# An encoder block on one core: transposed input, a late token factor for the first projections, and convolution weights split by adding transfers

## The chip, the cores and the metric

The kernel runs on one core of one Trainium2 chip, as one program. Its time is the device time of that core in microseconds (us). Three runs of the kernel before gave 2022.7, 2023.65 and 2024.65, so the median is 2023.65 us.

In the profile PE is TensorE's matmuls and PEld its weight loads, DVE is VectorE, ACT ScalarE, POOL GpSimd, SP SyncE. `L94` is line 94 of the kernel.

## What is computed

One layer on x of 512 tokens by 1024 channels, all in float32:

```
h   = x + Mixer(RMSNorm(x))
h   = h + PEER(RMSNorm(h))
out = RMSNorm_final(h)
```

The mixer multiplies the normalised x with one wide matrix `w_in` of 10,240 columns. Its columns go to a gated recurrence (HGRN2, 5 x 1024 columns), to a long convolution (Hyena: x0, x1 and v, 3 x 1024) and to two branch gates (2 x 1024). What this change touches is the norm, the convolution and one block of the second gate:

```python
def rmsnorm(x, g):
    y = xf * lax.rsqrt(jnp.mean(xf * xf, axis=-1, keepdims=True) + RMS_EPS)
    return y * g

proj = jnp.einsum('bld,dc->blc', xn, w_in)
q, zf_fwd, zf_bwd, inp, og, hy, gates = jnp.split(proj, IN_SPLITS, axis=-1)
hy = centred_short_conv(hy, conv_w, conv_b)
x0, x1, v = jnp.split(hy, 3, axis=-1)
y_b = x0 * bidirectional_fftconv(v * x1, h_f, h_b, hyena_bias)
```

The filters h_f and h_b come from a small network of sines. PEER is a product-key retrieval over 16,384 experts and takes the second half of the time; the change leaves its code alone.

## The kernel before

Numbers are held as a sum of two short ones: a high part that TensorE multiplies in one pass (dtype fp32r) and a low part, the residual. `split` (L91) makes them: ScalarE casts the high part, VectorE subtracts. `mm3` (L97) then multiplies high by high, low by high and high by low. A projection (`proj`, L144) computes 128 columns of `w_in` for all 512 tokens: `load_w` (L133) fetches a 512 KB weight block over SyncE's queue, splits it, and `product` (L149) runs 24 matmuls of 128x512 into one of three PSUM banks, named `ps_mm`.

**The start** (`mixer`, L217). x comes in four tiles of 128 tokens. For each, ScalarE squares it with a sum per token (`token_rstd`, L941), VectorE multiplies the tile with the token's factor and with the norm's gain, which TensorE had spread over the partitions (L243), and `turn` (L198) transposes it on TensorE, eight transposes per tile, and splits the result into `xh` and `xl`, the normalised input with channels on the partitions. The first two projections (`proj_halves`, L157) run on halves of the tokens between the transposes, 256 columns per matmul.

**The convolution** (`hyena`, L348). The 1024 channels go through in four rounds of 256, called `half` in the code. A round makes three projections for each of its two blocks of 128 channels: x1 (block 8 on), v (16 on) and x0 (0 on). `conv` (L374) is the centred short convolution on the projection's result: one ScalarE and two VectorE operations (L377 to L379), which also set the PSUM bank free. x1 times v is folded into `sd` (L539 to L543) and transposed on TensorE (L546, L558). `filtered` (L462) makes the round's filter, folds it (L493 to L509) and returns it; `parted` (L512) splits it into f0 and f1. `spectrum` (L574) multiplies with tables (`tco`, `tso`, ...), which come as transfers on GpSimd's queue that cast to fp32r (L398), each behind a copy of one column on ScalarE (L397), by which the moment of the transfer is set. Then come the products of the spectra, the way back and the multiplication with x0 (L648). Projections of the second gate fill in: `gates_b` (L261) yields one at a time.

**What sets the order.** The code is written stage by stage, and a scheduler puts the instructions of each engine into one row, in which they wait for each other's results. An engine takes its row strictly in that order; a transfer stands in the row of the engine that issues it. A tile of a pool can be filled again only when everything that used it is done. The weights had three raw tiles and two each for the high and the low part.

The lines that the prediction speaks of: L94 (the residual), L102 to L105 (`mm3`), L243, L250, L379, L398, L505 to L509, L546.

Of the kernel before, what the change touches and what calls it, by code (L numbers as in the profile page):

```python
# [9 lines left out]
F32 = mybir.dt.float32  # L10
# [31 lines left out]
for _n, _w in (("lb0", 8), ("lb1", 8), ("hg", 1), ("cw0", 24), ("cw1", 24), ("cw2", 24),  # L42
               ("cb", 24), ("f_b1", 1), ("f_q1", 1), ("f_b2", 1), ("f_q2", 1), ("negt", 4)):
    VEC[_n] = (_o, _w)
    _o += _w
# [80 lines left out]

def fetch_w(C, src):
    raw = C.wraw.tile([P, KB, P], F32, name="wraw")
    C.nc.sync.dma_start(raw, src)
    return raw  # L130


def load_w(C, src, raw=None, eng=None):  # L133
# [10 lines left out]
def proj(C, src, xh, xl, eng=None):  # L144

    return product(C, load_w(C, src, eng=eng), xh, xl)


def product(C, w, xh, xl):  # L149

    hi, lo = w
    ps = C.ps_mm.tile([P, L], F32, name="ps_mm")
    mm3(C.nc, ps, [((hi[:, k], lo[:, k]), (xh[:, k], xl[:, k])) for k in range(KB)])
    return ps

# [16 lines left out]
def block_kernel(tc, a):  # L172

    nc = tc.nc
    with ExitStack() as ctx:
# [5 lines left out]
        nc.scalar.dma_start(ident, a["ident"])  # L181
        epsc = const.tile([P, 1], F32, name="epsc")
        nc.vector.memset(epsc, EPS)
        C = Ctx()
        C.fetch_vec = lambda: nc.scalar.dma_start(vec, a["vec"])
# [27 lines left out]
FIRST_CONV = (8, 16)  # L213
# [3 lines left out]
def mixer(C):  # L217
# [3 lines left out]
    C.wraw = wctx.enter_context(tc.tile_pool(name="wraw", bufs=3))  # L221
    C.whi = wctx.enter_context(tc.tile_pool(name="whi", bufs=2))
# [7 lines left out]
    with tc.tile_pool(name="norm", bufs=1) as n1, tc.tile_pool(name="norm2", bufs=TB) as n2:  # L230
        log_table(C)
        C.fetch_vec()
        gm = n1.tile([1, D], F32, name="gm")
        gps = [C.ps_x.tile([P, 512], F32, name="ps_x") for _ in range(2)]
        xns, raws = [], []
        for tb in range(TB):
            xn = n2.tile([P, D], F32, name="xn")
            nc.sync.dma_start(xn, a["x"][tb * P : tb * P + P])
            xns.append(xn)
            if tb == 0:  # L240
                nc.scalar.dma_start(gm, a["g_mix"])
                for c, pg in enumerate(gps):
                    nc.tensor.matmul(pg, C.ones[0:1], gm[:, c * 512 : c * 512 + 512], start=True, stop=True)  # L243
            elif tb < 3:
                raws.append(fetch_w(C, a["w_in"][40 + FIRST_CONV[tb - 1]]))
        for tb, xn in enumerate(xns):
            rs = token_rstd(C, n2, xn, "nrs")
            for c, pg in enumerate(gps):
                xc = xn[:, c * 512 : c * 512 + 512]
                nc.vector.scalar_tensor_tensor(xc, xc, rs, pg, op0=ALU.mult, op1=ALU.mult)  # L250
            turn(C, xn, xh, xl, tb)
    rctx = ExitStack()
    branch = rctx.enter_context(tc.tile_pool(name="branch", bufs=1, side="right"))
    C.yb = mg = branch.tile([P, KB, L], F32, name="yb")
    gctx = ExitStack()
# [5 lines left out]
    def gates_b():  # L261
        w = None
        for db in range(KB):
# [11 lines left out]
    fill = gates_b()  # L275
    with ExitStack() as c2:
        hyena(C, c2, xh, xl, raws, fill)
# [51 lines left out]
def load_wo(C, pool, c):  # L329
# [7 lines left out]
    raw = C.wraw.tile([P, KB, P], F32, name="wraw")  # L337
    nc.sync.dma_start(raw, C.a["w_o"][c])
# [9 lines left out]
def hyena(C, ctx, xh, xl, raws, fill):  # L348
# [7 lines left out]
    w2 = ctx.enter_context(tc.tile_pool(name="hyw", bufs=2))  # L356
    HC = 256
# [13 lines left out]

    first = dict(zip(FIRST_CONV, proj_halves(C, (None, None), xh, xl, raws=raws)))

    def conv(dst, blk):  # L374

        ps = first.pop(blk, None) or proj(C, a["w_in"][40 + blk], xh, xl)
# [6 lines left out]
    alt = cp.tile([P, H + 2], F32R, name="alt")  # L383
    altc = cp.tile([P, 1], F32R, name="altc")

    def setup(steps):
# [7 lines left out]
        nc.sync.dma_start(fw2, a["f_w2"])  # L394
        for (name, w), step in zip(TABLES, steps):
# [66 lines left out]
    def filtered(half):  # L462

        hb = w2.tile([1, HC], F32, name="hb", bufs=1)
        nc.sync.dma_start(hb, a["hb"][:, half * HC : half * HC + HC])
        fw3 = w2.tile([2 * FH, 2, HC], F32, name="fw3", bufs=1)
# [3 lines left out]
        fw3h = w2.tile([2 * FH, 2, HC], F32R, name="fw3h", bufs=1)  # L470
        fw3l = w2.tile([2 * FH, 2, HC], F32R, name="fw3l", bufs=1)
# [3 lines left out]
        decb = w2.tile([P, 2, HC], F32, name="decb", bufs=1)  # L475
# [5 lines left out]
        pm_ = w2.tile([P, 2, 4, HC], F32, name="pm", bufs=1)  # L481
        for t in range(TB):
            win = w2.tile([P, 2, HC], F32, name="win")
# [8 lines left out]
            nc.vector.tensor_sub(pm_[:, 1, t], win[:, t // 2], win[:, 1 - t // 2])  # L492
        near, apart = pm_[0:1, 0], pm_[0:1, 1]  # L493
# [1134 lines left out]
```

## Time and profile before

The profiled execution took 2022.85 us, 0.8 less than the median of the runs. Its span, from the first to the last instruction, is 2021.1 us; 1.75 us lie around it.

| | us |
|---|---|
| median of 3 runs | 2023.65 |
| profiled execution | 2022.85 |
| its span | 2021.1 |
| mean granted TensorE clock | 0.995 |
| TensorE waiting for VectorE at L379, once | 7.1 |
| TensorE waiting before its first instruction | 6.1 |
| wlo, the weights' residuals on VectorE (112 in all) | 136.4 |

How to read it: a row of the waits names the engine and line that waited and what it waited for, with the total, the number of times and the longest. A table of stretches gives the busy time of each engine in each, with the number of instructions, then the clock that TensorE was granted (1.00 is full speed), the share of the transfer engines that was busy and what they moved. A row of the timeline has the start, the duration, the engine and line, what is written from what, and in brackets the idle time before it with what ended it. Matmuls overlap, so that 24 of 0.39 us follow each other at 0.227.

### The profile page before, as it was taken

What the parts mean: (1) busy time and instruction counts of PE and PEld (TensorE: products, weight loads), DVE (VectorE), ACT (ScalarE), POOL (GpSimd) and SP (SyncE); (2) the same over time, 40 slices, a digit from 0 to 9 for tenths busy, and PEclk for the clock granted to TensorE, in tenths of its full rate; (3) what the DMA queues carried; (4) which work ended last, traced back from release to release, by engine and by line L of the source; (5) the groups of instructions that cost most, each with busy time, mean ns of one, the idle gap of its engine ahead of it and who ended that gap; (6) DMA issues with size and microseconds to landing.
All of it is one profiled execution on the core that took longest, in us unless ns stands there. A gap on an engine that the chain in (4) does not pass through costs nothing.

```text
span 2021.1 us, 32312 instructions
## 1 busy us (share of the span) xinstructions
PE 1992.0 (99%) x12417; PEld 1760.2 (87%) x12417; DVE 1659.1 (82%) x2971; ACT 989.3 (49%) x1466; POOL 564.6 (28%) x338
## 2 busy tenths in 40 slices
PE   7989999999999999999999999999999999999998
PEld 6878888888888898889999998888888888888887
DVE  5799863889987737979999968877888889888995
ACT  5645453777775624436767643333333333333333
POOL 0000000000000000000000037777767767676760
PEclk9989999999999999999999999999999999999999
DMA  6412123222222434224767998889989899899984
GB/s 192 133 62 84 69 100 103 85 74 75 74 74 75 146 127 155 90 79 165 227 200 233 282 339 331 326 330 326 352 320 336 333 354 342 334 335 332 336 305 152
DMA packets 161683, 423.60 MB, mean 210 GB/s; under 512 B 12917, under 2 KB 64889, under 8 KB 161402
## 3 DMA queue, kind: packets, MB, share of 16 engines
q1 hardware_dynamic: 117176, 267.03, 37.9%
q0 software_dynamic: 37872, 137.91, 18.8%
q10 hardware_dynamic: 6482, 16.61, 2.4%
q8 instruction: 97, 1.59, 0.3%
q14 instruction: 56, 0.46, 0.1%
HBM read 381.92 MB, written 39.58 MB: 209 GB/s over the span
## 4 chain that ended last, share of the span: by engine, by line
PE 94%; DVE 4%; ACT 1%; DMA 1%; issue 1%; SPq 0%; DVEq 0%; ACTq 0%
PE ps_mm L105 10%; PE ps_mm L102 10%; PE ps_mm L103 10%; PE acc L1192 9%; PE acc L1191 9%; PE acc L1190 9%; PE ps_a L102 9%; PE ps_a L103 9%; PE ps_a L105 8%; PE ps_g L1477 4%; PE ps_x L748 1%; PE ps_x L102 1%; PE ps_x L105 1%; PE ps_x L103 1%; PE ps_s L1322 1%
## 5 line engine op out<-in xcount | busy, mean ns | idle before, releaser
L94 POOL TENSOR_TENSOR ul<-uraw,uh 128x1024 fp32r<-128x1024 f32 x70 | 186.7, 2667 | 576.1 <-PE ps_a L105 436.3
L102 PE MATMUL ps_a<-pxh,uh 128*128 128x384 f32 x1024 | 345.8, 338 | 0.3 <-ACT gact L1042 0.3
L103 PE MATMUL ps_a<-pxl,uh 128*128 128x384 f32 x1024 | 342.3, 334 | 0.0
L1192 PE MATMUL acc<-vh,gl 128*128 128x512 f32 x768 | 300.7, 392 | 0.0
L1191 PE MATMUL acc<-vl,gh 128*128 128x512 f32 x768 | 300.0, 391 | 0.0
L1190 PE MATMUL acc<-vh,gh 128*128 128x512 f32 x768 | 299.2, 390 | 0.0
L102 PE MATMUL ps_mm<-xh,whi 128*128 128x512 f32 (+1 forms) x656 | 257.8, 395 | 7.1 <-DVE x L379 7.1
L93 ACT CAST vh<-vraw 128x1024 fp32r<-128x1024 f32 x128 | 134.6, 1052 | 256.5 <-PE acc L1192 137.2
L103 PE MATMUL ps_mm<-xl,whi 128*128 128x512 f32 (+1 forms) x656 | 255.4, 391 | 0.0
L1145 DVE SCALAR_TENSOR_TENSOR xg<-grow,gw,xg 128x1024 f32<-128x1024 f32 x127 | 201.8, 1589 | 27.4 <-DMA grow<-in_v,gidx 25.8
L1133 DVE SCALAR_TENSOR_TENSOR grow<-grow,xg 128x1024 f32<-128x1024 f32 x128 | 187.0, 1480 | 44.9 <-DMA grow<-in_u,gidx 44.6
L1104 POOL DMA_INDIRECT grow<-in_u,gidx x128 | 198.5, 1551 | 36.4 <-issue 22.9
L105 PE MATMUL ps_a<-pxh,ul 128*128 128x384 f32 x1024 | 198.4, 334 | 0.0
L102 PEld LDWEIGHTS ps_a<-pxh,uh 128*128 128x128 f32 x1024 | 192.4, 188 | 3.7 <-ACT gact L1042 0.6
L103 PEld LDWEIGHTS ps_a<-pxl,uh 128*128 128x128 f32 x1024 | 192.4, 188 | 3.7
L1013 POOL IOTA iota<- 128x512 bf16 x1 | 1.2, 1190 | 691.4 <-PE ps_mm L105 691.4
L93 ACT CAST uh<-uraw 128x1024 fp32r<-128x1024 f32 x128 | 134.7, 1052 | 119.7 <-PE ps_a L103 83.2
L94 DVE TENSOR_TENSOR wlo<-wraw,whi 128x1024 fp32r<-128x1024 f32 x112 | 136.4, 1219 | 68.8 <-ACT whi L93 39.4
L94 DVE TENSOR_TENSOR vl<-vraw,vh 128x1024 fp32r<-128x1024 f32 x128 | 186.8, 1460 | 6.2 <-ACT vh L93 6.2
L1104 POOL DMA_INDIRECT grow<-in_v,gidx x128 | 174.2, 1361 | 36.7 <-issue 20.9
L105 PEld LDWEIGHTS ps_a<-pxh,ul 128*128 128x128 f32 x1024 | 179.3, 188 | 0.0
L93 ACT CAST whi<-wraw 128x1024 fp32r<-128x1024 f32 x112 | 117.3, 1048 | 120.6 <-PE ps_mm L103 108.1
(427 smaller groups left out, 3952.3 us busy)
## 6 DMA issues: line engine op xcount, KB each, us to landing
uraw<-in_uT SPq DMA_DIRECT2D x128, 512.0 KB, 5.7
vraw<-in_v SPq DMA_DIRECT2D x128, 512.0 KB, 6.0
wraw<-in_w_in SPq DMA_DIRECT2D x80, 512.0 KB, 3.3
Gd<-Gs SPq DMA_DIRECT2D x12, 2048.0 KB, 10.1
gt<-Gd SPq DMA_DIRECT2D x32, 768.0 KB, 7.8
kept<-gact ACTq DMA_DIRECT2D x22, 384.0 KB, 2.9
gkept<-kept SPq DMA_DIRECT2D x22, 384.0 KB, 5.6
wraw<-in_w_q SPq DMA_DIRECT2D x16, 512.0 KB, 4.2
```

Source lines behind the costliest of these rows:

```text
L93: nc.scalar.copy(hi, src)
L94: return (eng or nc.vector).tensor_sub(lo, src, hi).ins
L102: nc.tensor.matmul(out, ah, bh, start=(i == 0), stop=False)
L103: nc.tensor.matmul(out, *((al, bh) if late else (ah, bl)), start=False, stop=False)
L105: nc.tensor.matmul(out, *((ah, bl) if late else (al, bh)), start=False, stop=(stop and i == n - 1))
L1104: nc.gpsimd.indirect_dma_start(out=t, out_offset=None, in_=tab, in_offset=bass.IndirectOffsetOnAxis(ap=gidx[:, j : j + 1], axis=0))
L1133: nc.vector.scalar_tensor_tensor(t, t, 1.0, xg, op0=ALU.mult, op1=ALU.mult, accum_out=gdot[h][:, i : i + 1])
L1145: nc.vector.scalar_tensor_tensor(gacc, t, gw[h][:, i : i + 1], gacc, op0=ALU.mult, op1=ALU.add)
L1190: nc.tensor.matmul(acc[k][c], gh[:, ts_], vh[:, ds_], start=(r == 0), stop=False)
L1191: nc.tensor.matmul(acc[k][c], gh[:, ts_], vl[:, ds_], start=False, stop=False)
L1192: nc.tensor.matmul(acc[k][c], gl[:, ts_], vh[:, ds_], start=False, stop=(r == NK - 1))
L1477: nc.tensor.matmul(pg[:, q * P : q * P + P], own[:, q], rows[:, q], start=True, stop=True)
```

## The change

Eight things change, three of them large.

1. **The input comes transposed as well** (`xT`, laid out on the host), in eight slices of 128 channels by 512 tokens. There are no transposes in the mixer any more. The new function `begun` scales each slice with the norm's gain alone (`gm`, one number per channel) and splits it into `uh` and `ul`.
2. **The first five projections multiply `uh` and `ul`** and get the token's factor `rs` afterwards, by one multiplication of the result. They are the first block of the second gate, which stood in the first round, and the four convolution blocks of the list `FIRST_CONV`: 8, 16, 0 and 9. The factor comes from the sum of the squares of the slices, made by ScalarE and VectorE and summed over the partitions by one fp32 matmul with ones (L259). Meanwhile VectorE and ScalarE make `xh` and `xl` from the slices for all later projections. The results lie in `yb`, which the convolution fills only later: the gate's is stored from there, and `conv` reads the other four.
3. **The convolution's weights are split by transfers.** While `C.cast` is set, a transfer on GpSimd's queue casts the weight into the high part (L145), ScalarE writes its negative into the low part (L146), and a second transfer of the same 512 KB adds the weight to it (L147). VectorE has no part in it. After the convolution weights are split as before.
4. The pools of raw, high and low tiles become one ring of seven tiles of the same size. A raw tile takes the place of a low part of three weights before.
5. The folding of the filter (`folded_filter`) is cut from `filtered` and done where its result is split, so in the next round behind the convolutions.
6. The alternating signs come cast on GpSimd's queue too, and the tables' marker copies read other tiles.
7. `ident` is fetched later, some tiles of `hyena` lie in a pool of their own.
8. The halves of the first two projections are gone: all matmuls of a projection have 512 columns.

The core of the difference:

```diff
 def load_w(C, src, raw=None, behind=None):
     nc = C.nc
+    if raw is None and C.cast:
+        hi, lo = w_tile(C, "whi"), w_tile(C, "wlo")
+        if behind is not None:
+            nc.scalar.copy(hi[:, 0, 0:1], behind)
+        nc.gpsimd.dma_start(hi, src)
+        nc.scalar.mul(lo, hi, -1.0)
+        nc.gpsimd.dma_start(lo, src, accum_op=ALU.add)
+        return hi, lo
     if raw is None:
         raw = fetch_w(C, src)
-    hi = C.whi.tile([P, KB, P], F32R, name="whi")
-    lo = C.whi.tile([P, KB, P], F32R, name="wlo")
-    split(nc, hi, lo, raw, eng)
+    hi, lo = w_tile(C, "whi"), w_tile(C, "wlo")
+    split(nc, hi, lo, raw)
     return hi, lo
...
+def begun(C, xh, xl):
...
+        raw, w = w_tile(C, "wraw", F32), (w_tile(C, "whi"), w_tile(C, "wlo"))
+        for k in range(KB):
+            if k in (0, KB // 2):
+                ks = slice(k, k + KB // 2)
+                nc.sync.dma_start(raw[:, ks], a["w_in"][72][:, ks])
+                split(nc, w[0][:, ks], w[1][:, ks], raw[:, ks])
+            nc.sync.dma_start(xT[:, k], a["xT"][:, k])
+        later = fetch_w(C, a["w_in"][40 + FIRST_CONV[0]])
+        C.fetch_ident()
+        for k in range(KB):
+            g = vcol(C, "gm", k)
+            nc.scalar.activation(uh[:, k], xT[:, k], AF.Identity, scale=g)
+            nc.vector.scalar_tensor_tensor(ul[:, k], xT[:, k], g, uh[:, k], op0=ALU.mult, op1=ALU.subtract)
+        gate0 = product(C, w, uh, ul, C.ps_x, "ps_x")
+        made = {}
+        w = load_w(C, None, later)
+        total = sp.tile([P, L], F32, name="total", bufs=1)
+        nc.scalar.activation(total, xT[:, 0], AF.Square)
+        for k in range(1, KB):
+            sq = sp.tile([P, L], F32, name="sq")
+            nc.scalar.activation(sq, xT[:, k], AF.Square)
+            nc.vector.tensor_add(total, total, sq)
+        ms = C.ps_x.tile([P, L], F32, name="ps_x")
+        nc.tensor.matmul(ms, C.ones, total, start=True, stop=True)
+        rstd_from(C, rs, ms, 1.0 / D)
+        for i, blk in enumerate(FIRST_CONV):
+            if i:
+                w = load_w(C, a["w_in"][40 + blk], behind=xT[:, KB - 1, 0:1])
+            made[blk] = product(C, w, uh, ul)
...
+                nc.vector.tensor_mul(yb[:, 3 + i], made[blk], rs)
...
+        evict(0)
+        for k in range(KB):
+            nc.vector.scalar_tensor_tensor(xT[:, k], xT[:, k], vcol(C, "gm", k), rs, op0=ALU.mult, op1=ALU.mult)
+            C.turned = nc.scalar.copy(xh[:, k], xT[:, k]).ins
+            nc.vector.tensor_sub(xl[:, k], xT[:, k], xh[:, k])
+        evict(1)
+    return evict, gate0
-FIRST_CONV = (8, 16)
+FIRST_CONV = (8, 16, 0, 9)
...
-    C.wraw = wctx.enter_context(tc.tile_pool(name="wraw", bufs=3))
-    C.whi = wctx.enter_context(tc.tile_pool(name="whi", bufs=2))
+    C.ring = wctx.enter_context(tc.tile_pool(name="weights", bufs=7))
+    C.cast = True
...
+        return lambda: folded_filter(pm_, hb)
...
         if half == 1:
-            fe, fo = parted(*folded)
+            fe, fo = parted(*rest())
...
-        if half < 2:
+        if half == 1:
             next(fill)
```

The rows of three engines show what the scheduler made of it. First ScalarE at the start. Before, casts of the transposed input (`xh`) stand between the squares of the tiles (`junk`):

```order
L124 ACTIVATE nrs<-nrs 128x1
L93 CAST whi<-wraw 128x1024
L209 CAST xh<-ps_x 128x4x128
L945 ACTIVATE junk,nrs<-xn 128x1024
L209 CAST xh<-ps_x 128x4x128 x3
L123 ACTIVATE nrs<-nrs,epsc 128x1
```

Now, behind the last scaled slice (`sq` is a slice's square, `whi<-xT` the marker of a cast transfer, `wlo<-whi` the negative, `yb` the token factor's logarithm, L123, and exponential, L124):

```order
L247 ACTIVATE uh<-xT,vec 128x512 x3
L256 ACTIVATE sq<-xT 128x512 x2
L93 CAST whi<-wraw 128x1024
L256 ACTIVATE sq<-xT 128x512
L144 CAST whi<-xT 128x1
L256 ACTIVATE sq<-xT 128x512 x2
L146 ACTIVATE wlo<-whi 128x1024
L123 ACTIVATE yb<-ps_x,epsc 128x512
L144 CAST whi<-xT 128x1
L124 ACTIVATE yb<-yb 128x512
L276 CAST xh<-xT 128x512
L448 COPY signs<-xh 128x1
```

The negative of the first cast weight, which needs that weight's transfer, stands ahead of the token factor and of the next weight's marker. Second, GpSimd, whose row in the convolution held the seven tables:

```order
L398 DMA tco<-in_tco 128x1024
L398 DMA tso<-in_tso 128x1024
L398 DMA tee<-in_tee 128x1024
L398 DMA tceT<-in_tceT 128x1032
L398 DMA tsoT<-in_tsoT 128x1032
```

Now the cast (L145) and adding (L147) transfers stand between them, with numbers to tell the weights apart:

```order
L145 DMA whi_216<-in_w_in 128x1024
L147 DMA wlo_217<-in_w_in 128x1024
L145 DMA whi_247<-in_w_in 128x1024
L449 DMA signs_352<-in_alt 128x259
L453 DMA tco_512<-in_tco 128x1024
L147 DMA wlo_248<-in_w_in 128x1024
L145 DMA whi_278<-in_w_in 128x1024
L453 DMA tso_515<-in_tso 128x1024
L145 DMA whi_410<-in_w_in 128x1024
L147 DMA wlo_279<-in_w_in 128x1024
```

The high part of a later weight stands ahead of the low part of an earlier one: 410 ahead of 279. Third, VectorE at the end of the first round and in the second. Before, the folding of the next filter (`pm_875`, `once_919`) stands ahead of the convolutions of the second block (`x1_1129`, `vv_1131`, out of the PSUM banks 1138 and 1172):

```order
L505 TENSOR_TENSOR once_919<-pm_875 128x1024
L554 TENSOR_TENSOR tw_1084<-ps_x_1075,far_1082 128x2x128
L506 TENSOR_TENSOR pm_875<-pm_875 128x2x512
L94 TENSOR_TENSOR uel_996<-tw_1084,ueh_995 128x4x128
L508 TENSOR_TENSOR pm_875<-once_919 128x2x256
L509 TENSOR_TENSOR pm_875<-once_919 128x2x256
L370 TENSOR_TENSOR um_322<-ps_x_1090,um_322 1x128
L378 SCALAR_TENSOR_TENSOR x1_1129<-ps_mm_1138,vec_61,x1_1129 128x511
L378 SCALAR_TENSOR_TENSOR vv_1131<-ps_mm_1172,vec_61,vv_1131 128x511
L379 SCALAR_TENSOR_TENSOR x1_1129<-ps_mm_1138,vec_61,x1_1129 128x511
L379 SCALAR_TENSOR_TENSOR vv_1131<-ps_mm_1172,vec_61,vv_1131 128x511
L94 TENSOR_TENSOR wlo_1230<-wraw_1227,whi_1229 128x1024
```

Now the same block's convolution (`vv_1045`, out of bank 1084) comes first:

```order
L609 TENSOR_TENSOR tw_999<-ps_x_990,far_997 128x2x128
L432 SCALAR_TENSOR_TENSOR vv_1045<-ps_mm_1084,vec_61,vv_1045 128x511
L703 TENSOR_TENSOR yb_87<-yconv_903,x0_469 128x512
L94 TENSOR_TENSOR uel_913<-tw_999,ueh_912 128x4x128
L590 TENSOR_TENSOR x1_1043<-vv_1045,x1_1043 128x512
L431 SCALAR_TENSOR_TENSOR x0_1138<-ps_mm_1144,vec_61,x0_1138 128x511
```

and the folding (`pm_808`, `once_1182`) follows 20 rows further on, right ahead of the split of the filter (`f1l`, `f0l`) for the next spectrum:

```order
L560 TENSOR_TENSOR once_1182<-pm_808 128x1024
L561 TENSOR_TENSOR pm_808<-pm_808 128x2x512
L563 TENSOR_TENSOR pm_808<-once_1182 128x2x256
L564 TENSOR_TENSOR pm_808<-once_1182 128x2x256
L94 TENSOR_TENSOR f1l_1191<-pm_808,f1h_1190 128x1024
L94 TENSOR_TENSOR f0l_1189<-pm_808,f0h_1188 128x1024
```

The folding has moved behind the convolutions, and no residual of a weight (`wlo`) is left in this part of VectorE's row.

More of the change, by code (lines that the diff above doesn't have):

```diff
@@ L184, in block_kernel @@
         C = Ctx()
+        C.fetch_ident = lambda: nc.scalar.dma_start(ident, a["ident"])
         C.fetch_vec = lambda: nc.scalar.dma_start(vec, a["vec"])
@@ L210, in turn, with evict @@
         nc.vector.tensor_sub(xl[:, ks, ts_], src, xh[:, ks, ts_])
-FIRST_CONV = (8, 16)
+def begun(C, xh, xl):
+    nc, tc, a = C.nc, C.tc, C.a
+    yb = C.yb
+    rs = yb[:, KB - 1]
+    with tc.tile_pool(name="raw", bufs=1, side="right") as rp, tc.tile_pool(name="square", bufs=2, side="right") as sp:
+        xT = sp.tile([P, KB, L], F32, name="xT", bufs=1)
+        uh = rp.tile([P, KB, L], F32R, name="uh")
+        ul = rp.tile([P, KB, L], F32R, name="ul")
+        log_table(C)
+        C.fetch_vec()
+        raw, w = w_tile(C, "wraw", F32), (w_tile(C, "whi"), w_tile(C, "wlo"))
[27 more added lines that the diff above has]
+            made[blk] = product(C, w, uh, ul)
+        def evict(i):
+            blk = FIRST_CONV[i]
+            if made[blk] is not None:
+                nc.vector.tensor_mul(yb[:, 3 + i], made[blk], rs)
+                made[blk] = None
+            return yb[:, 3 + i]
+        evict(0)
[5 more added lines that the diff above has]
+    return evict, gate0
@@ L229, in mixer @@
     xl = xp.tile([P, KB, L], F32R, name="xl")
[L230 to L251, printed above, removed]
     rctx = ExitStack()
@@ L254, in mixer @@
     C.yb = mg = branch.tile([P, KB, L], F32, name="yb")
+    evict, gate0 = begun(C, xh, xl)
+    first = {blk: lambda i=i: evict(i) for i, blk in enumerate(FIRST_CONV)}
     gctx = ExitStack()
@@ L262, in gates_b @@
         w = None
-        for db in range(KB):
+        graw = C.yb[:, 2]
+        nc.vector.tensor_mul(graw, gate0, C.yb[:, KB - 1])
+        nc.sync.dma_start(C.gbd[0], graw)
+        yield
+        for db in range(1, KB):
             now = w or load_w(C, a["w_in"][72 + db])
@@ L275, in mixer @@
     fill = gates_b()
+    next(fill)
     with ExitStack() as c2:
-        hyena(C, c2, xh, xl, raws, fill)
+        hyena(C, c2, xh, xl, first, fill)
+    C.cast = False
     with tc.tile_pool(name="gb", bufs=1) as cp:
@@ L336, in load_wo @@
     o = (c - first) * P
-    raw = C.wraw.tile([P, KB, P], F32, name="wraw")
-    nc.sync.dma_start(raw, C.a["w_o"][c])
+    raw = fetch_w(C, C.a["w_o"][c])
     split(nc, hi[:, :, o : o + P], lo[:, :, o : o + P], raw)
@@ L474, in filtered @@
         nc.vector.tensor_sub(fw3l, fw3, fw3h)
-        decb = w2.tile([P, 2, HC], F32, name="decb", bufs=1)
+        decb = w3.tile([P, 2, HC], F32, name="decb", bufs=1)
         with tc.issue_after(C.turned):
@@ L480, in filtered @@
             nc.scalar.activation(decb, decb, AF.Abs)
-        pm_ = w2.tile([P, 2, 4, HC], F32, name="pm", bufs=1)
+        pm_ = w3.tile([P, 2, 4, HC], F32, name="pm", bufs=1)
         for t in range(TB):
-            win = w2.tile([P, 2, HC], F32, name="win")
+            win = w3.tile([P, 2, HC], F32, name="win")
             nc.scalar.activation(win, decb, AF.Exp, scale=vcol(C, "negt", t))
@@ L503, in filtered @@
         lower, upper = pm_[:, :, 0:2], pm_[:, :, 2:4]
-        once = w2.tile([P, 2, 2, HC], F32, name="once", bufs=1)
+        once = w3.tile([P, 2, 2, HC], F32, name="once", bufs=1)
         nc.vector.tensor_add(once, lower, upper)
@@ L562, in hyena @@
         if half == 1:
-            fe, fo = parted(*folded)
+            fe, fo = parted(*rest())
         nc.scalar.copy(uo[0][0:1, 0], um[0:1])
@@ L622, in hyena @@
         if half < D // HC - 1:
-            folded = filtered(half + 1)
+            rest = filtered(half + 1)
         for j in range(NJ):
@@ L1565, in layout @@
     out["x"] = ca(x)
+    out["xT"] = ca(x.T.reshape(KB, P, L).transpose(1, 0, 2))
     cols = lambda w, width: ca(w.reshape(KB, P, -1, width).transpose(2, 1, 0, 3))
@@ L1600, in layout @@
     put("hg", A["hgrn_norm_g"][0])
+    put("gm", A["norm_mix_g"])
     for j in range(3):
```

67 lines of the change are left out of this document (33 added, 34 removed).

## The prediction

> **What bounds the kernel now.** I read the page first, then TensorE's waits, then a table of stretches over the first 330 us. The page says that TensorE is busy nearly all of the 2021.1 us:
>
> ```profile
> PE 1992.0 (99%) x12417; PEld 1760.2 (87%) x12417; DVE 1659.1 (82%) x2971; ACT 989.3 (49%) x1466; POOL 564.6 (28%) x338
> ```
>
> So taking work off VectorE gains nothing by itself. Only 29 us of idle TensorE, and stretches at a lower clock, can be won. TensorE's longest waits (total, times, longest):
>
> ```profile
> PE ps_mm L102 <- DVE x L379: 7.1, 1, 7.1
> PE ps_x L243 <- DMA gm<-in_g_mix: 6.1, 1, 6.1
> PE ps_x L546 <- DVE sd L539: 4.3, 3, 3.8
> ```
>
> They lie in the first 136 us, in the norm and the convolution's first half. I cut the stretches at these waits:
>
> ```profile
> core 0: us, PE busy (x) PEld busy (x) DVE busy (x) ACT busy (x) POOL busy (x), PEclk, DMA share, GB/s
> 0.00:14.77 14.77, 7.51 (x21) 4.30 (x21) 5.97 (x13) 10.55 (x20) 0.20 (x4) 1.00 0.78 293
> 14.77:28.76 13.99, 13.99 (x113) 13.84 (x113) 10.65 (x18) 5.78 (x11) 0.72 (x1) 1.00 0.45 130
> 28.76:37.07 8.31, 4.50 (x21) 3.39 (x20) 4.30 (x7) 5.00 (x9) 0.00 (x0) 0.95 0.61 176
> 37.07:42.89 5.82, 5.82 (x16) 4.65 (x17) 3.74 (x10) 2.16 (x6) 0.55 (x1) 0.50 0.26 62
> 47.10:52.54 5.44, 5.44 (x25) 4.50 (x24) 2.63 (x3) 1.83 (x2) 0.35 (x1) 1.00 0.82 235
> 59.35:93.50 34.15, 34.05 (x150) 27.69 (x148) 29.24 (x57) 22.15 (x37) 1.39 (x3) 1.00 0.51 154
> 93.50:122.70 29.20, 29.16 (x191) 25.76 (x189) 26.91 (x54) 16.62 (x33) 0.00 (x0) 1.00 0.09 28
> 122.70:129.82 7.12, 0.00 (x0) 0.00 (x1) 7.07 (x12) 3.41 (x5) 0.00 (x0) 0.66 0.00 0
> 129.82:135.78 5.96, 5.96 (x18) 4.45 (x18) 5.42 (x9) 1.51 (x3) 0.00 (x0) 0.55 0.27 91
> 135.78:330.00 194.22, 193.96 (x1048) 166.63 (x1047) 143.32 (x238) 91.06 (x159) 0.00 (x0) 1.00 0.27 90
> ```
>
> 47.10:52.54 is one projection: 24 matmuls in 5.44 us, 0.227 each. 0.00:14.77 is the start, with no projection in it. 122.70:129.82 is the longest wait: TensorE does nothing while VectorE is busy 7.07 of 7.12 us, so it waits for a VectorE that is behind. Behind this wait the granted clock (PEclk) is 0.55 for 5.96 us, which costs another 2.7; behind the one of 3.8 it is 0.50 for 5.82 us, which costs 2.9. From 135.78 on TensorE has no gap left (193.96 of 194.22).
>
> The Trainium skill ("TensorE: Matmul & The Clock Gate", Part 1) says that TensorE falls to half rate after an idle window of about 3.4 us; both waits, 3.8 and 7.1, agree. The change makes new waits of nearly that length.
>
> **The change part by part.** The sum is made against the profiled execution, 2022.85 us (span 2021.1), 0.8 under the median of 2023.65; gains go over one to one.
>
> *Start, until two projections are done.* Before, that is at 28.76, with 10.9 us of products in it: 17.9 us go to the start, to transposes among the products and to halved matmuls. The prices for the new start:
>
> ```profile
> 4.60 1.06 ACT L945 ACTIVATE junk<-xn 128x1024 f32<-128x1024 f32 x1 [2.11 <-DMA xn<-in_x]
> ...
> 10.01 2.72 DVE L250 SCALAR_TENSOR_TENSOR xn<-xn,nrs,ps_x 128x512 f32<-128x512 f32 x4
> ...
> 33.02 0.71 ACT L484 ACTIVATE win<-decb,vec 128x512 f32<-128x512 f32 x1
> 33.63 0.76 ACT L377 ACTIVATE vv<-ps_mm,vec 128x512 f32<-128x512 f32 x1
> 34.30 0.71 ACT L484 ACTIVATE win<-decb,vec 128x512 f32<-128x512 f32 x1
> 34.91 1.03 ACT L93 CAST whi<-wraw 128x1024 fp32r<-128x1024 f32 x1
> ```
>
> The first 512 KB were there at 4.60; now they are half a weight and one slice of the input. After one square ScalarE makes the first scaled slice from 5.3 (the vector of scales may come as late as gm did, 6.1). Eight scalings, two squares and half a cast stand in its row up to the last slice: 10 x 0.65 (33.02 to 34.30 is two) + 0.5, so 12.4. VectorE's residual (0.7) ends at 13.1, and eight low products (1.8) at 15. The second projection's cast comes behind two squares, 12.4 + 1.3 + 1.0 = 14.7, so it follows on at once. With one fp32 product of the sums (about 0.9, four times 0.227) and a short wait for the last sum it ends at 22.4, 6.4 us ahead of before.
>
> *Three more projections, with cast and adding transfers.* Transfers on GpSimd's queue (issue to landing), one issue, and the transposes of a block:
>
> ```profile
> tco<-in_tco POOLq DMA_DIRECT2D x1, 512.0 KB, 7.9
> tso<-in_tso POOLq DMA_DIRECT2D x1, 512.0 KB, 3.9
> tcoT<-in_tcoT POOLq DMA_DIRECT2D x1, 512.0 KB, 4.8
> ...
> 40.21 0.55 POOL L398 DMA_DIRECT2D tso<-in_tso  x1 [17.38 <-ACT tso L397]
> ...
> 57.48 0.52 PE L546 MATMUL ps_x<-ident,sd 128*128 128x128 f32 x3
> 57.84 0.27 PE L558 MATMUL ps_x<-ident,sd 128*128 128x128 f32 x1
> ```
>
> The high part is such a cast transfer; I take 4.8. No row shows an adding one. It reads the tile as well, so it hardly takes less than 3.9; as two of the slowest it would take 15.8. I take 6, halfway between the rows 3.9 and 7.9.
>
> Weight 16's high part is asked at 16 (its marker stands behind squares on ScalarE), lands at 21, is negated (1.05) by 22.3, and its low part lands at 28.3. TensorE does the 16 high products from 22.4 to 26.0, waits 2.3, ends at 30.1. Behind ScalarE's wait for that landing stand the logarithm and exponential of the token factor, so the factor is there at 23.8 instead of 20.6, and the next weight's marker: weight 0's high part is asked at 23.1, lands at 27.9, is negated by 29.0, its low part lands at 35.0; TensorE is there at 33.7, waits 1.3, ends at 36.8. Weight 9: asked 29.2, landed 34.0, negated behind the eight casts of xh at 35.0, low part 41.0; TensorE waits 0.6 and ends at 42.8. Five projections at 42.8 stand against four and five transposes (0.6) at 47.10: 4.3 + 5.44 - 0.6 = 9.1 ahead. With 7.9 for an adding transfer the end is 44.7, and some 3 us of waits follow in the next four weights: 4 ahead. With 3.9 it is 12.
>
> VectorE has 35 operations at 0.68 (the row at 10.01) and 2.4 of wlo from 5.5 on, 26 us, with its waits over by about 38; the transposes of the first block have 12 more rows ahead of them, come at about 45 and may cost a wait of 0 to 2. I keep **8 us** (4 to 12).
>
> *The wait of 7.15.* VectorE's part in it (wlo alone, and the folding, which ran in the wait):
>
> ```profile
> 59.35:129.70 70.35, 14.99 (x56) 10.44 (x56) 7.28 (x6) 0.97 0.28 86
> ...
> L506 DVE TENSOR_TENSOR pm<-pm 128x1024 f32<-128x1024 f32 x1 | 1.2, 1203 | 0.0
> L505 DVE TENSOR_TENSOR once<-pm 128x1024 f32<-128x1024 f32 x1 | 1.2, 1200 | 0.0
> ...
> L508 DVE TENSOR_TENSOR pm<-once 128x512 f32<-128x512 f32 x1 | 0.7, 674 | 0.0
> ...
> L509 DVE TENSOR_TENSOR pm<-once 128x512 f32<-128x512 f32 x1 | 0.7, 671 | 0.0
> ```
>
> The six wlo (7.28) are gone. VectorE had 4.9 us of idle time in 59.35:93.50, which hid up to three of them, so 3.6 to 7.3 count. The folding, 3.8, now stands behind the convolutions that TensorE waited for. Together 7.4 to 11.1 against 7.1: the wait goes, and the low clock behind it. What is late next is that folding, ahead of the next spectrum: about 18.6 us of VectorE rows against 81 matmuls, 18.4 us. So I leave 2 of 7.1 + 2.7 as waits: **8 us** (3 to 10).
>
> *Later cast weights.* The ring of seven tiles lets a high part be asked three projections ahead (16.3), and the low part is wanted 3.6 later: 19.9 - 4.8 - 1.05 - two issues of 0.55 leaves 13 us for an adding transfer. At 6 nothing waits, and GpSimd has no other work there.
>
> *Later weights without a cast.*
>
> ```profile
> wraw<-in_w_a SPq DMA_DIRECT2D x8, 512.0 KB, 3.8
> ```
>
> The raw tile now waits for a product where it waited for a split. At w_a, with w_o's tiles in the same ring, its lead is 1.8 + 5.44 = 7.3 us, for 3.8 of landing and 1.05 of cast in a shared row. I take **1 us** lost (0 to 3).
>
> 8 + 8 - 1 = 15 us: 2023.65 - 15 = 2009 us.
>
> The Trainium skill ("DMA: Bandwidth & Descriptors", Anatomy of one DMA) prices a transfer on this path at 2.0 us plus bytes over 436 GB/s. Estimated by that, 512 KB take 3.2 us and twice the bytes 4.4; the trace's rows, 3.9 to 7.9, are all longer. By 4.4 the start would gain about 11, and the time be 2006.
>
> **Rivals.**
>
> *Slow adding transfers: slower than before.* If one takes over 13 us, each of 21 later cast weights makes TensorE wait in mid-projection. At 13 the start has lost about 6, and the sum, -6 + 8 - 1, is near no change; each us above costs 21. At 15.8 the start loses 12: 2023.65 + 12 - 8 + 1 + 21 x 2.8 = 2087. For it: no row shows this form. Against: the slowest row of its queue is 7.9. 0.12.
>
> *The clock stays low in the start.* TensorE is fed a pair of products every 0.7 to 0.9 us there and then meets waits of up to 2.3. If 32 matmuls of the first two projections run at clock 0.5 (0.227 more each), that costs 7 of the 8: 2016. For it: 0.50 behind the wait of 3.8. Against: 1.00 in 14.77:28.76, behind a start just as sparse. 0.15.
>
> *The VectorE wait moves.* TensorE waits for the folded filter ahead of the spectrum as long as it did for the convolution, clock included: 8 - 1, 2016.5. For it: 18.6 against 18.4 is no margin. Against: VectorE comes there 3.6 or more lighter. 0.13.
>
> *Nothing waits at all* (transfers at 3.9, all of the 9.8): 12 + 10 - 1, 2002.5. 0.08.
>
> **How the numbers follow.** The forecast, 2009, has 0.52. The range, 2001 to 2020, takes in the second and third rival and most of the last; the first and mixtures are left out, about 0.18. A measurement of this kernel can tell 0.2%, 4 us, from no change. Faster by more (under 2019.6): 0.52 + 0.08 and most of 0.15 + 0.13, 0.79. Slower by more: 0.12. The rest, 0.09, is a loss in the start that eats the other gain.
>
> **What would show it.** Right: the first projection's matmuls begin near 6 us, two projections are done by 22 to 24, five by 41 to 45; TensorE's waits for adding transfers are 1 to 3 us each and lie in the first 60 us; no wait for a convolution above 2 us; the first spectrum begins near 86 us. Wrong: adding transfers that land after more than 8 us (the start) or 13 (all), a granted clock of 0.50 between 22 and 45 us, or a long wait of TensorE for the folded filter.

## The result, and the profile after

The changed kernel took 2040.92 us (median of five runs, 2035.3 to 2048.57), the kernel before 2022.89 beside it. The ratio is 1.0091, with a 95% interval of 1.0064 to 1.0118: **18 us slower**, where 2009 and a gain of 14 had been forecast. It also spreads more: 13 us between its five runs, 2 in those of before. Run once more later, it took 2045.67 (2035.7 to 2053.2).

The page of the profiled execution (2040.92 us, span 2039.2) says where to look. VectorE has 20 us less to do, and TensorE, though it was given fewer instructions, is busy 5 us longer and idle 13 us longer (2039.2 - 1997.0 against 2021.1 - 1992.0). All of it lies ahead of the experts' half, whose first products with the keys (`ps_s`) begin at 789.77 instead of 770.59, with 1249 and 1250 us behind them:

```profile
PE 1997.0 (98%) x12335; PEld 1761.7 (86%) x12335; DVE 1638.8 (80%) x2963; ACT 987.0 (48%) x1470; POOL 607.5 (30%) x397
```

TensorE's waits (total, times, longest), the largest:

```profile
PE ps_x L601 <- DVE sd L594: 8.4, 5, 3.2
PE ps_x L102 <- ACT uh L247: 6.3, 1, 6.3
PE ps_mm L105 <- DMA wlo<-in_w_in: 5.8, 3, 2.6
PE ps_x L601 <- ACT sd L596: 4.2, 1, 4.2
PE ps_x L102 <- ACT f1h L93: 3.9, 2, 2.6
...
PE ps_x L958 <- ACT o L952: 1.9, 1, 1.9
PE ps_x L946 <- ACT sct L936: 1.8, 1, 1.8
```

The 7.1 us for a convolution's last step is gone, as forecast. In its place stand many waits of 1.3 to 4.2 us, for the folded input (`sd`), for the filter's high part (`f1h`) and for low parts of weights (`wlo`). The stretches show where they lie; two projections were done at 24.08, five at 46.92, and the first spectrum began at 101.96:

```profile
0.00:24.08 24.08, 17.66 (x51) 11.34 (x51) 14.93 (x26) 16.15 (x27) 2.42 (x7) 1.00 0.53 175
24.08:46.92 22.84, 18.79 (x73) 14.44 (x72) 16.93 (x31) 9.87 (x19) 6.96 (x11) 0.93 0.94 245
46.92:101.96 55.04, 46.02 (x195) 36.73 (x193) 33.55 (x74) 31.05 (x56) 13.60 (x20) 0.93 0.88 222
62.16:68.40 6.24, 6.24 (x19) 5.17 (x20) 2.70 (x7) 3.78 (x10) 1.07 (x2) 0.60 1.01 289
101.96:109.00 7.04, 7.04 (x34) 6.85 (x35) 4.87 (x7) 3.54 (x5) 0.88 (x1) 0.56 0.84 189
109.00:188.68 79.68, 75.32 (x441) 65.03 (x440) 64.88 (x123) 42.51 (x82) 10.00 (x14) 1.00 0.45 107
188.68:280.00 91.32, 86.34 (x467) 74.38 (x468) 63.65 (x120) 41.13 (x77) 12.31 (x17) 0.94 0.49 116
262.86:269.50 6.64, 6.64 (x27) 5.84 (x28) 3.38 (x9) 3.42 (x7) 0.00 (x0) 0.57 0.22 44
280.00:330.00 50.00, 50.00 (x247) 42.25 (x247) 25.07 (x37) 21.07 (x33) 0.00 (x0) 1.00 0.32 111
```

Up to 46.92 the new start is ahead, as forecast. Between there and 101.96 nine of 55 us are idle, and the clock (PEclk) is near a half behind two of the waits. From 109 to 280 another 9.3 us are idle; before, TensorE had no gap behind 135.78. VectorE is not what is late: it is busy 64 of 91 us in 188.68:280.

What is late is ScalarE, and one place shows how. The timeline of the last wait, with GpSimd's issues of an adding transfer and of the cast transfer ahead of it:

```profile
251.80 0.88 POOL L147 DMA_DIRECT2D wlo<-in_w_in  x1 [3.73 <-ACT wlo L146]
252.35 0.89 POOL L145 DMA_DIRECT2D whi<-in_w_in  x1
```

```profile
258.45 1.06 ACT L146 ACTIVATE wlo<-whi 128x1024 fp32r<-128x1024 f32 x1 [6.29 <-DMA whi<-in_w_in]
...
259.42 0.76 ACT L430 ACTIVATE vv<-ps_mm,vec 128x512 f32<-128x512 f32 x1
...
260.21 0.75 DVE L431 SCALAR_TENSOR_TENSOR vv<-ps_mm,vec,vv 128x511 f32<-128x511 f32 x1 [6.48 <-ACT vv L430]
...
262.51 0.30 DVE L594 TENSOR_TENSOR sd<-x 128x129 f32<-128x129 f32 x1
...
262.86 0.47 PE L601 MATMUL ps_x<-ident,sd 128*128 128x128 f32 x1 [3.24 <-DVE sd L594]
...
277.10 0.39 PE L102 MATMUL ps_mm<-xh,whi 128*128 128x512 f32 x1
```

ScalarE came to the negation of a weight (L146) with 6.29 us to wait for a cast transfer issued at 252.35. The convolution's eviction (L430) stood behind it in the row, though its projection had been done at about 256. VectorE and TensorE only pass that delay on: VectorE sits idle 6.48 us, and TensorE is told to wait for VectorE's `sd`. Nothing needed the negation so early: the next product with a new weight begins at 277.10. GpSimd's row adds to it: the cast transfer is issued right behind an adding one, which had itself waited 3.73 us for the negation before. 20 of the 29 cast transfers are issued within 1.5 us behind an adding one, so the two rows wait for each other. ScalarE's waits for transfers in the first 330 us, before and after:

```profile
ACT alt L402 <- DMA scratch<-in_alt: 3.9, 1, 3.9
...
ACT fw3h L473 <- DMA fw<-in_f_w: 3.2, 1, 3.2
...
ACT decb L480 <- DMA decb<-in_f_decay: 2.4, 2, 1.3
```

```profile
ACT wlo L146 <- DMA whi<-in_w_in: 32.2, 13, 6.3
ACT whi L93 <- DMA wraw<-in_w_b: 22.9, 6, 5.2
...
ACT decb L531 <- DMA decb<-in_f_decay: 11.4, 4, 6.0
```

The sum of ScalarE's waits is not the point. Before, it waited longer, for products to let a weight tile go, and no wait of TensorE's there names such a cast:

```profile
ACT whi L93 <- PE ps_mm L103: 52.8, 24, 4.4
```

What matters is what stands behind a wait. So theory 1: **ScalarE's row stands still at transfers, and the convolution's pieces behind it come late.** Theory 2, the rival from the prediction: the later folding of the filter makes VectorE late. Theory 3: the adding transfers land too late for the products themselves.

### The profile page after: what moved, and what is told of

Same layout as the page of the kernel before. It is cut to its first block, busy times and chain, and to the rows that moved or that the text cites. A ratio compares the mean times of both kernels' runs of the same rounds, so it can differ in the third digit from the quotient of the medians.

```text
span 2039.2 us, 32177 instructions
## 1 busy us (share of the span) xinstructions
PE 1997.0 (98%) x12335; PEld 1761.7 (86%) x12335; DVE 1638.8 (80%) x2963; ACT 987.0 (48%) x1470; POOL 607.5 (30%) x397
## 4 chain that ended last, share of the span: by engine, by line
PE 85%; issue 6%; DMA 3%; DVE 2%; ACT 2%; POOL 1%; SPq 0%; ACTq 0%; DVEq 0%; POOLq 0%
PE ps_a L103 9%; PE ps_a L102 9%; PE ps_a L105 9%; PE acc L1245 9%; PE acc L1246 9%; PE acc L1247 9%; PE ps_mm L105 8%; PE ps_mm L102 8%; PE ps_mm L103 8%; PE ps_g L1532 4%; DMA wraw<-in_w_in 1%; PE ps_s L1377 1%; PE ps_x L803 1%; DMA whi<-in_w_in 1%; DMA decb<-in_f_decay 1%
## 5 line engine op out<-in xcount | busy, mean ns | idle before, releaser
L102 PE MATMUL ps_mm<-xh,whi 128*128 128x512 f32 x600 | 242.9, 405 | 0.0
L103 PE MATMUL ps_mm<-xl,whi 128*128 128x512 f32 x600 | 235.9, 393 | 0.9 <-issue 0.9
L1200 DVE SCALAR_TENSOR_TENSOR xg<-grow,gw,xg 128x1024 f32<-128x1024 f32 x127 | 208.0, 1638 | 27.3 <-DMA grow<-in_v,gidx 25.3
L1159 POOL DMA_INDIRECT grow<-in_u,gidx x128 | 191.6, 1497 | 42.0 <-issue 20.1
L1159 POOL DMA_INDIRECT grow<-in_v,gidx x128 | 182.8, 1428 | 35.3 <-issue 17.9
L94 DVE TENSOR_TENSOR vl<-vraw,vh 128x1024 fp32r<-128x1024 f32 x128 | 178.2, 1392 | 4.9 <-ACT vh L93 4.8
L1247 PEld LDWEIGHTS acc<-vh,gl 128*128 128x128 f32 x768 | 144.2, 188 | 30.6
L1245 PEld LDWEIGHTS acc<-vh,gh 128*128 128x128 f32 x768 | 144.2, 188 | 28.1
L1246 PEld LDWEIGHTS acc<-vl,gh 128*128 128x128 f32 x768 | 144.2, 188 | 27.4
```

The lines of the kernel that those rows point to most:

```text
L94: return (eng or nc.vector).tensor_sub(lo, src, hi).ins
L102: nc.tensor.matmul(out, ah, bh, start=(i == 0), stop=False)
L103: nc.tensor.matmul(out, *((al, bh) if late else (ah, bl)), start=False, stop=False)
L1159: nc.gpsimd.indirect_dma_start(out=t, out_offset=None, in_=tab, in_offset=bass.IndirectOffsetOnAxis(ap=gidx[:, j : j + 1], axis=0))
L1200: nc.vector.scalar_tensor_tensor(gacc, t, gw[h][:, i : i + 1], gacc, op0=ALU.mult, op1=ALU.add)
L1245: nc.tensor.matmul(acc[k][c], gh[:, ts_], vh[:, ds_], start=(r == 0), stop=False)
```

## The experiments

Times are medians, each beside before's 2022.7 to 2023.7 in the same call, with the interval of the ratio to before. Executions of the changed kernel and its near relatives differ by up to 10 us and more, so single steps under 5 us aren't told apart.

**The negation later.** The list `C.evicted` takes each ScalarE eviction of a projection:

```diff
-        nc.scalar.mul(lo, hi, -1.0)
+        with C.tc.issue_after(C.evicted[-2]) if len(C.evicted) >= 2 else nullcontext():
+            nc.scalar.mul(lo, hi, -1.0)
```

> The changed kernel, with one thing altered: ScalarE's negation of a cast weight is ordered behind its eviction of the projection two before, instead of where the scheduler put it (ahead of evictions that TensorE's transposes wait for). Theory 1, ScalarE's row stands still at a negation whose cast transfer has not landed, and convolution and filter behind it come late: TensorE's waits of 1.31 us at 149.05, 2.69 at 188.68, 1.73 at 243.83 and 3.24 at 262.86 go, with the half clock behind them (1.7 and 3.4), so 14 us less than the 2040.9 of the changed kernel: 2027 (2022 to 2032). Theory 2, VectorE's later folding of the filter makes those waits: no change, 2038 to 2044. Theory 3, the adding transfers land too late for the products: their start is put off further, so more waits at the low products and a time over 2044.

2030.89 us (1.0023 to 1.0057), 10 less. TensorE's time in the stretch where the waits of 2.69, 1.73 and 3.24 us had been:

```profile
150.00:280.00 130.00, 129.87 (x762) 112.73 (x761) 104.71 (x194) 67.83 (x128) 17.47 (x24) 1.00 0.54 129
```

No gap is left, with the same transfers, the same bytes and the folding where the change had put it. Of the forecast 14 us 10 came; theory 1 holds for this stretch, and theories 2 and 3 fall for it.

**The first round's decay rates early.**

```diff
-        with tc.issue_after(C.turned):
+        with tc.issue_after(C.turned) if half else nullcontext():
-                (nc.sync if half else nc.scalar).dma_start(decb[:, dr], ...)
+                nc.sync.dma_start(decb[:, dr], ...)
```

> The changed kernel, with one thing altered: the first round's decay rates (decb, two transfers of 128 KB) are asked for on SyncE's queue, where they stand near its start, instead of in ScalarE's row at 52.8 and 53.6 us. Theory 1 (ScalarE's row stands still at transfers): its wait of 5.99 us for decb goes, and with it TensorE's wait of 4.22 us for sd at 62.16 and the half clock behind it (3.4): 7.6 us less than 2040.9, 2033 (2030 to 2037). If that wait was not what held TensorE: 2038 to 2044.

2042.83 (1.0088 to 1.0119): no gain, a miss. The wait of 4.22 us at 62.16 went, but the next one grew from 2.63 to 4.86 us:

```profile
98.00 0.39 PE L102 MATMUL ps_x<-f1h,tco 128*128 128x256 f32 x1 [4.86 <-ACT f1h L93]
```

In its profile the same product of the experts' half began 4.9 us sooner than in the changed kernel's (778.64 and 783.49), which the end did not show: from the first products with the keys on, that execution took 1255.2 us, the changed kernel's 1249.4. (In the second run of this edit it was 1249.3, so the loss there was not the edit's.) So both were run again on one chip, after the next experiment had shown what the two edits do together.

> The changed kernel as it is, for comparison on the same chip: 2036 to 2045.

> The changed kernel with the first round's decay rates asked for early, again. In its profile the experts' first product came 4.9 us sooner than in the changed kernel's. If that stands: 4 to 6 us under after_again. If what is won there is lost again: within 2 us of it.

2045.67 (1.0083 to 1.0116) and 2038.12 (1.0068 to 1.0093): 7.5 less here, with intervals that overlap. Alone, its worth between 0 and 8 stays open.

**Both together.**

> The negation behind the eviction of the projection two before, and the first round's decay rates asked for early on SyncE's queue, together. With the first alone (2030.9) TensorE still waited 5.28 us at 64.75 for sd, which stood behind ScalarE's wait for decb, with half clock for 6.8 us behind it. Theory 1: these 8.7 us go, less 2 to 3 that the next filter's wait takes: 2024 (2021 to 2028). Rival, what follows (f1h) is late anyway and takes all of it, as with the second alone: 2029 to 2033.

2021.74 (0.9983 to 1.0001), 9 less than the later negation alone and 19 less than the change. With the negations behind ready evictions and the first decay rates early, the change costs nothing any more. The stops themselves are not gone: up to 330 us ScalarE still waits 14.7 us for cast transfers (32.2 in the changed kernel) and 5.0 for decay rates (11.4). They hold up less.

**Plain transfers for the adding ones**, run once and then timed:

```diff
-        nc.gpsimd.dma_start(lo, src, accum_op=ALU.add)
+        nc.gpsimd.dma_start(lo, src)
```

> The changed kernel with a plain cast transfer in the place of each adding one, so the low part holds the weight itself and the residual is left out; order and bytes stay. If adding is what takes time (5.3 to 7.2 us from the issue to the product that waited for it), TensorE's waits at low products fall from 5.8 us to under 2. If an adding transfer takes no longer than a plain one beside another of the same size, they stay at 4 to 7.

> The run with plain transfers in the place of the adding ones once more, now timed (the low part holds the weight itself). The single time was 2017.4, beside 2040.9 with adding ones in the same rows. If it stands: 2014 to 2021, so what the adding itself costs (1.4 us more to landing, 1.6 more for the cast transfer behind it) becomes some 23 us through the rows that wait. If that single run was a lucky one: over 2030.

2017.44 and 2018.79 (0.9967 to 0.9988), 22 less, with the rows of the four compute engines the same. The values differ, but the 22 us lie ahead of the experts' half, which takes 1249.5 us (1249.4 in the changed kernel). The transfers by issue, with the median from issue to landing: first with adding (from the later negation's run, where the trace has landings), then plain:

```profile
whi<-in_w_in POOLq DMA_DIRECT2D x29, 512.0 KB, 6.4
wlo<-in_w_in POOLq DMA_DIRECT2D x29, 512.0 KB, 5.5
```

```profile
whi<-in_w_in POOLq DMA_DIRECT2D x29, 512.0 KB, 4.8
wlo<-in_w_in POOLq DMA_DIRECT2D x29, 512.0 KB, 4.0
```

An adding transfer took 1.5 us longer to land than a plain one, and the cast transfers, most of them issued right behind one (26 of 29 in that run), 1.6 longer. TensorE's waits at low products fell from 5.8 to 2.1 us (1.55 and 0.59), which is 4 of the 22. ScalarE's waits at negations fell too, to 19.6 from 32.2. That the rest of the 22 hangs on these is argued from the place above, not shown wait by wait.

```profile
ACT wlo L146 <- DMA whi<-in_w_in: 19.6, 11, 4.2
```

**No cast at all**: the new start, the ring and the later folding, with `C.cast = False`.

> The changed kernel, but every convolution weight is split by ScalarE and VectorE from a raw tile as before; start, ring of seven tiles and later folding stay. VectorE gets 28 residuals of 1.2 us back. Theory 1 (ScalarE waits for cast transfers): the 14 us of waits behind negations and the 7.5 us at low products go, some of VectorE's old wait (7.1 + 2.7) may come back: 2020 to 2030. Theory 2 (VectorE's later folding is the cause): a VectorE with 34 us more to do is later still, 2045 or more. Theory 3 (only the adding transfers' landing): the 7.5 us go, 2033.

2024.49 (1.0001 to 1.0019). So the cast with its adding transfers costs 16 of the 18 us, net of what it spares VectorE. Theory 2 had expected more time here.

**The later folding alone, on the kernel before** (`filtered` returns `lambda: folded_filter(pm_, hb)`, `parted` calls it).

> The kernel before, with one part of the change alone: the folding of the next filter is cut off and done where its result is split. Theory 1 (the folding is harmless): TensorE's wait of 7.1 us for VectorE's convolution shrinks by the folding's 3.8 and the half clock behind it falls, 3 to 9 us less than before, 2014 to 2020. Theory 2 (the folding moves the wait to the filter): a wait of TensorE for f1h or sd takes its place, no gain or slower, 2022 to 2030.

2024.13 (0.9995 to 1.0013): no change, a miss for theory 1's number. Where TensorE had waited 7.1 us, 1.5 for a low part are left, but other waits came instead:

```profile
PE ps_x L550 <- DVE sd L543: 8.1, 3, 4.6
...
PE ps_mm L105 <- DVE wlo L94: 1.7, 2, 1.5
...
PE ps_mm L102 <- DVE x L379: 1.5, 1, 1.5
PE ps_x L550 <- DVE sd L546: 1.1, 1, 1.1
```

VectorE's arrears weren't worked off, they were met 50 us later, in the next round (waits of 1.5, 3.3 and 1.1 us from 171 to 180).

**The new start alone, and with the later folding.** Both split all weights as before, in the old pools; the second folds later. The change's smaller items (6 and 7) are in both.

```diff
+    return (C.wraw if name == "wraw" else C.whi).tile([P, KB, P], dt, name=name)
```

> The kernel before with the new start alone: transposed input, five products of the unnormalised slices, the token factor afterwards, 512 columns throughout. Weights are split by ScalarE and VectorE in the old pools (three raw, two high, two low), and the filter is folded in its old place. Theory 1 (the start gains, what follows it in the changed kernel loses): some 5 to 9 us less than before, 2014 to 2018. Rival, TensorE only comes earlier to the place where it waits for VectorE (7.1 us before), so that this wait grows by what the start gained: 2020 to 2025.

> The new start, all weights split by ScalarE and VectorE, the old pools, and the later folding. Counterpart of the run above. If the later folding costs the 11 us: 2021 to 2026. If the ring does: 2012 to 2017. The later folding alone on the kernel before changed nothing (2024.1 beside 2022.7), which speaks for the ring.

2013.28 and 2014.42 (both 0.9941 to 0.9968). The start is worth 10 us, and the folding again nothing. These two beat both kernels. In the second, VectorE's old wait stands at full length, 50 us further on:

```profile
178.81 0.77 PE L102 MATMUL ps_mm<-xh,whi 128*128 128x512 f32 x1 [7.58 <-DVE x L433]
```

**The ring.** Old folding with the ring; a ring of six; and three raw tiles apart from a ring of four for the rest. None casts.

> The new start, all weights split by ScalarE and VectorE, the ring of seven tiles, and the filter folded in its old place. The same with the later folding took 2024.5, and with old folding and old pools (three raw, two high, two low) 2013.3: 11 us lie between them. If the later folding costs them: 2012 to 2017. If the ring does (a raw tile waits for a product and comes late to ScalarE's cast): 2021 to 2026. If both: between.

> The new start, all weights split by ScalarE and VectorE, the later folding, and a ring of six tiles instead of seven (with seven: 2024.5). If the ring costs by the lead that its tiles give a raw weight, one tile less puts each raw transfer off by part of a projection, ScalarE waits for it longer, and the time rises to 2035 or more. If the ring's size is not what costs: 2022 to 2027.

> The new start, all weights split by ScalarE and VectorE, the later folding, and the same seven tiles, but three of them a pool for raw weights alone and four a ring for high and low parts. With one ring of seven: 2024.5; with pools of three, two and two: 2014.4. If a raw tile's place behind a product costs (it is fetched only when a product has let a tile go, and ScalarE's cast waits for it): 2012 to 2017. If it is the sharing of high and low parts: 2021 to 2027.

2032.12 (1.0021 to 1.0049), 2028.21 (1.0016 to 1.0035) and 2024.33 (0.9998 to 1.0016). With either folding the ring costs: 2024.5 against 2014.4, 2032.1 against 2013.3. And with the ring the later folding is worth 7.6 us (2032.1 against 2024.5), which it is not without. The obvious reason, that raw weights come late to ScalarE's cast, does not carry it. ScalarE's waits for them up to 750 us, with one ring of seven and with raw tiles apart:

```profile
ACT whi L93 <- DMA wraw<-in_w_in: 45.7, 25, 4.6
```

```profile
ACT whi L93 <- DMA wraw<-in_w_in: 1.8, 1, 1.8
```

They went, and the time stayed. In their place ScalarE waits 82.7 us for products to let a tile go, much as with the old pools (78.7 in the run with start and folding). One tile less in the ring added 3.7 where 10 had been expected. The ring also brought the change's waits in the recurrence, behind 600 us: one for `sct` is there in the run without a cast (2.5 us), and not with the old pools. Shown is that one ring of four for high and low parts, in the place of two and two, is enough to lose 10 us (2024.3 against 2014.4). The traces of these two show the first link. Up to 38 us their rows are the same, within 1 us. Then ScalarE's cast of the weight after next stands in another place of its row, first with the old pools, then with the ring of four, where it comes behind the decay rates:

```profile
38.85 1.05 ACT L93 CAST whi<-wraw 128x1024 fp32r<-128x1024 f32 x1 [0.54 <-PE ps_mm L103]
```

```profile
48.17 1.03 ACT L93 CAST whi<-wraw 128x1024 fp32r<-128x1024 f32 x1
```

With the old pools TensorE does that weight's high products meanwhile and then waits 0.50 us for a low part. With the ring it stands:

```profile
48.05 3.55 PE L105 MATMUL ps_mm<-xh,wlo 128*128 128x512 f32 x8 [4.14 <-DVE wlo L94]
```

High and low tiles are always taken in pairs, so four shared tiles should come round in the same order as two and two. This speaks for the scheduler's order as the cause, and not for a tile that comes free late. That is argued, not shown, and the later links, and the chain in the ring of seven, stay open: each change of a pool reorders rows.

**Cast where VectorE is behind.** From the later negation's kernel: old folding, and cast weights in the second round alone (`C.cast = half == 1`).

> The changed kernel with cast and adding transfers for the weights of the convolution's second round alone, the negation ordered behind the eviction of the projection two before, the filter folded in its old place, and all other weights split by ScalarE and VectorE. VectorE is rid of some seven residuals (8.5 us) just where TensorE waited for it before. Theory 1: start's 5 and the old wait's 7.1 + 2.7 are won, less 2 for the ring: 2011 (2006 to 2017). Rival, low parts that land late and the ring's short lead eat it: 2018 to 2026.

2029.82 (1.0021 to 1.0048), a miss. The arrears came all the same, where VectorE's residuals begin again:

```profile
182.14 0.79 PE L105 MATMUL ps_mm<-xh,wlo 128*128 128x512 f32 x1 [9.63 <-DVE wlo L94]
```

**GpSimd takes residuals** in the second and third rounds, on top of the new start (`split(nc, hi, lo, raw, C.residual)`).

> The new start with old pools and old folding (2013.3), with one thing more: the residuals of the weights made in the convolution's second and third rounds are taken by GpSimd, which has no other work there, instead of VectorE. If VectorE's arrears are what still holds TensorE in these rounds (waits of 2.19, 1.36 and 4.01 us at 129.7, 162.8 and 170.7, and half clock for 6.8 us), some 7 go: 2006 (2003 to 2010). Rival: GpSimd takes twice VectorE's time for a residual (2.65 beside 1.2 us in the experts' half), low parts come late and TensorE waits for them: 2013 to 2020.

2032.71 (1.0031 to 1.0058), 19 slower than without: a miss. While GpSimd took a residual, VectorE's folding, 1.20 us elsewhere, took 3.09:

```profile
133.06 3.43 POOL L94 TENSOR_TENSOR wlo<-wraw,whi 128x1024 fp32r<-128x1024 f32 x1 [11.69 <-ACT whi L93]
```

```profile
134.48 3.09 DVE L563 TENSOR_TENSOR pm<-pm 128x1024 f32<-128x1024 f32 x1
```

The Trainium skill ("GPSIMD Engine Reference", 1. Specifications) says that GpSimd shares its SBUF interfaces with VectorE and contends with instructions that have two SBUF inputs; the folding is one, and these rows agree. VectorE's rows with an operand from PSUM kept their time beside a residual (0.75 us for L433 at 199.37), while most that read SBUF alone stood until GpSimd was done (an operation of 0.28 us took 2.02 at 139.72). Where VectorE had begun first, GpSimd lost: 3.43 us at 133.06 instead of 2.4. From 55 to 260 us VectorE's rows grew by some 25 us in all (an estimate, each row's mean against the run without), and 15 residuals of 1.2 us, 18 in all, were what it was spared.

## Why the prediction was wrong

The runs give a chain of medians for the parts: before 2022.9; the start, -9.6 (2013.3); the later folding, +1.1 (2014.4); the ring, +10.1 (2024.5); the cast, +16.4 (2040.9). The steps depend on their order, as the 7.6 us of the folding with the ring show.

*The start, 8 forecast (4 to 12): right.* By itself it gained 9.6. In the changed kernel it had some 5 when five projections were done, at 46.92 and not 42.8: the waits for the three low parts were 0, 1.5 and 2.6 us (2.3, 1.3 and 0.6 forecast), and the clock stood at half behind the last (0.53 for 3.43 us, one of the signs that the prediction had named for being wrong).

*The adding transfer, 6 forecast: right, 5.5.* TensorE met only three waits for low parts, two in the start and one of 1.78 us (at 78.34) in the later weights, where the budget of 13 us had said none. The rival of slow adding transfers, which needed over 13, fell.

*The step that failed* is "At 6 nothing waits, and GpSimd has no other work there". The budget asked only whether TensorE would wait for a low part. It did not ask what stands behind the negation in ScalarE's row. At the start the prediction had asked that very question, of the token factor behind the first negation, and the row of ScalarE shown ahead of it has the form; for the later weights it was dropped. Nor did GpSimd's row stand free: its cast transfers wait behind adding ones, and these for negations. A cast transfer landed in 6.4 us, not the 4.8 taken; beside plain transfers in the same rows it was 4.8. The scheduler had put the negation ahead of evictions that were ready first. Price: 10 us (later negation), 19 with the decay rates, the other transfer at which ScalarE's row stood.

*The decay rates were missed.* The rows of before had them asked at 22 us, 9 us ahead of their use (31.5); the change moved the issue in ScalarE's row behind the casts of the slices and the first convolutions, to 53, and ScalarE then waited 5.99 us for the landing. A transfer that an engine issues stands in that engine's row too, and this one wasn't looked up.

*VectorE's wait, 8 forecast.* It did go, and the run without a cast speaks for VectorE's lost residuals as the reason: with them back, TensorE is idle 10.7 of the 79 us from 109 to 188, 3.7 in the changed kernel. The part credited to the folding was wrong: alone it gains nothing and the wait moves, on the kernel before to `sd` and with the new start to a convolution 50 us on; not to the folded filter, as that rival had it. Only with the ring is it worth something, 7.6 us.

*The ring, -1 forecast (0 to 3): mis-sized, 10 (19 with the old folding).* Only the one place (w_a) was looked at.

*The clock in the start*: 1.00 up to 24.08, so that rival fell for the two projections it was about.

The range ended at 2020 because slowness was given one mechanism only, landings of over 13 us, and these were 5.5.

## What to carry to other kernels

A split that is moved from an engine to transfers leaves one small instruction on another engine that waits for a transfer, and in a row taken strictly in order everything behind it waits too: look at what stands behind it, for every weight, and order it behind work that is ready first, above all where nothing needs its result soon. A named wait may be the last link: TensorE waited "for VectorE" while VectorE sat idle behind ScalarE. Take the parts of a change apart: here the start alone (2013.3 us) was worth more than the whole.

## What the runs showed of the hardware that was not expected

An adding cast transfer of 512 KB took 5.5 us to land against 4.0 for a plain one, 0.88 us of GpSimd's time to issue against 0.53 (medians), and it slowed its neighbours: cast transfers 6.4 against 4.8.

Half clock followed shorter waits than the 3.8 us seen before. Behind a wait of 2.59 us:

```profile
43.49:46.92 3.43, 3.43 (x8) 2.71 (x9) 0.33 (x2) 0.00 (x0) 0.00 (x0) 0.53 1.06 247
```

Behind 2.63 us (101.96:109.00 above) it lasted twice as long. The Trainium skill ("TensorE: Matmul & The Clock Gate", Part 1) names an idle window of about 3.4 us; no idle time of that length stands directly ahead of these two, so here less than one such window was enough. The length alone does not decide: behind a wait of 1.98 us (cast in the second round alone, 64.38) the clock was 0.54 for 3.6 us, and behind one of 1.99 (later negation, 80.70) it stayed at 1.00.
